# Gaps in SBUF that set where the streamed operands of single-pass matmuls lie against the weights loaded beside them

## The chip, the cores and the metric

One core of one Trainium2 chip runs the whole program. The metric is device time in microseconds (us), lower is better. TensorE's matmul array is PE, its weight loads are PEld; DVE is VectorE, ACT is ScalarE, POOL is GpSimd, and SP is the queue that issues most loads.

## The reference

256 tokens of 1,024 values pass through a first block (a mixer of attention and a state recurrence, then product-key experts) and a second block of two layers (feed-forward, mixer, feed-forward each). All is float32. The parts with most products:

```python
def peer_ffn(h, w_query, sub_keys1, sub_keys2, expert_u, expert_v):
    q = x @ w_query                                    # 8 heads, top 16 of 128*128 experts each
    ...
    u = jnp.take(expert_u, ic, axis=0)
    act = jax.nn.gelu(jnp.einsum('cd,ced->ce', xc, u))
    vv = jnp.take(expert_v, ic, axis=0)
    return jnp.einsum('ce,ced->cd', gc * act, vv)

def swiglu(h, w_gate, w_up, w_down):                   # four of them; 1024 x 2816, 2816 x 1024
    return (jax.nn.silu(h @ w_gate) * (h @ w_up)) @ w_down
```

## The kernel before

Every large product is made of single-pass matmuls in the type float32r, whose operands are split in two parts that add up to the float32 value: `mm3` (L105 to L107) issues three matmuls, of high by high, high by low and low by high part. One matmul loads 128x128 weights into the array and streams an operand [128, 256] past them, the transposed activations of all 256 tokens (in `proj_n` the roles are swapped). While one streams, the weights of the next are loaded, so at any time two places of SBUF are read for TensorE: the streamed operand of this matmul and the weights of the next.

The stages, in order of time, with the streamed operand and the weights by their tile names:

- `first_half`: the products with `w_in` (`xh`, `xl` against `wh`, `wl`), then the recurrence, attention and `w_out` (`qk..`, `zr..` against `wh`, `wl`), woven together.
- `peer`: the query products (`xh`, `xl` against `wh`, `wl`). Then the **u stage**, 128 blocks of 128 experts each: SP loads a block of `peer_u` (tile `u`, two buffers), DVE transposes it (`uT`), ACT and POOL split it (`uh`, `ul`, three buffers), and PE does 24 matmuls (`ph`, `pl` against `uh`, `ul`). Beside it DVE finds the best keys, and from the middle on `spread` builds the gates from one-hot tiles (`one`, DVE and ACT), multiplies them on PE (L1148, two-pass float32 matmuls of 128 columns) and applies them (`G`, DVE). DVE, ACT and POOL keep their written order here. Then the **v stage**, again 128 blocks of 24 matmuls (L1291 to L1293): SP loads two blocks at a time (tile `v`, two buffers, L1270), ACT, DVE and POOL split them (`vh`, `vl`, L1277 and L1278), ACT and DVE split the gated activations (`ah`, `al`), and PE streams `ah`, `al` against `vh`, `vl`. All eight sums stay in PSUM through the stage.
- The second block: `ffn` four times. Its gate and up products stream `xh`, `xl` (44 groups of 24 matmuls), its down product streams `hh`, `hl` (528 matmuls, L1340 on, eight sums in four pairs). Between them the mixers (`mxh`, `mxl`; `grr`, `gir`).

Tiles come from pools that lie one behind the other in a partition; a pool's memory is given to the next pool when it closes, and an instruction that writes a tile waits for the readers and writers of whatever lay there before. So the size of every tile ahead of another in a pool sets that tile's address, and with it what its first write waits for. The order of instructions on an engine is set by the tile scheduler and, within `peer`, by the program.

Of the kernel before, what the change touches and what calls it, by code (L numbers as in the profile page):

```python
# [26 lines left out]
HOLD = 1.5  # L27
HALVES = slice(0, 64), slice(64, 128)


class K:
    """What the parts of the program share."""
# [30 lines left out]
    def pw(self, shape):  # L63
        """A bank from both of the working tags in turn."""
        self.turn = (self.turn + 1) % 3
        return self.psum(shape, tag="o", bufs=2) if self.turn == 2 else self.psum(shape)

    def raws(self, es, bufs=3):
        """Room for weights as they come, as long as es lasts."""
        self.raw = es.enter_context(self.tc.tile_pool(reuse_waits="tile", name="raw", bufs=bufs))  # L70

    def splits(self, es, bufs=3, width=1024):
        """Room for the parts of weights, as long as es lasts."""
# [9 lines left out]
    def load(self, src, k0, nk, n0, n):  # L83
        """Rows k0*128.. of src [K, N], columns n0..n0+n, with the rows on partitions."""
# [7 lines left out]
    def split(self, v):  # L92
        """Two parts that add up to the weights [128, nk, n]."""
# [8 lines left out]
    def mm3(self, out, sh, sl, mh, ml, first, last):  # L102
        """out += s.T @ m from the parts of both."""
# [9 lines left out]
    def columns_of(self, R, name):  # L113
        """R, the same in every partition, with the tokens on partitions: [128, 2]."""
# [13 lines left out]
class Rms:  # L128
    """1/sqrt(mean(x^2) + eps) over the rows of xT, the same in every partition: [128, T]; chunk by chunk as x comes."""
# [6 lines left out]
    def chunk(self, c):  # L136
# [12 lines left out]
        if c == self.early:  # L149
            # the table that the root needs  # L150
# [20 lines left out]
class Norm(Rms):  # L171
    """x * g in two parts, and what rmsnorm scales the tokens by; if by4 the parts' tokens are chunked()."""
# [24 lines left out]
class Last:  # L197
    """The rows of x by tokens, rmsnorm and the way out."""
# [9 lines left out]
    def chunk(self, c):  # L208
# [8 lines left out]
        if c == 6:  # L217
            # the table that the root needs
# [15 lines left out]

def weave(nc, tasks):
    """Emits generators side by side: of those whose last step should be through first, the first in the list takes its next
    step. tasks are (name, generator, names it comes behind)."""
# [33 lines left out]
# ---------------------------------------------------------------- first block  # L271
def columns(k, pool, rows, name, eng=None):
    """Vectors as rows of 128 -> columns over partitions."""
# [16 lines left out]
def vec(ap):  # L290
    """A flat vector of n*128 as [n, 128]."""
    return ap.rearrange("(n p) -> n p", p=128)


def modulation(k, pool, px):
    """silu(c) @ ada_w + ada_b, as columns [128, 48]: the first third, and generators for the others."""
# [59 lines left out]
def modulated(k, pool, tmp, g, shift, scale, R):  # L356
    """x R g (1 + scale) + shift in two parts."""
# [15 lines left out]
def proj_t(k, w, xh, xl, n0, n, use, nk=8, k0=0):  # L373
    """(x @ w[:, n0:n0+n]).T in chunks of 128 rows: use(chunk, psum [128, T])."""
# [20 lines left out]
def proj_n(k, w, xh, xl, n0, n, use, nk=8):  # L395
    """x @ w[:, n0:n0+n] by token tiles: use(tile, column, psum [128, 256])."""
# [20 lines left out]
def rsqrt(k, new, p, scale, eps):  # L417
    """1/sqrt(scale*p + eps), or of max(p, eps) without a scale; one Newton step behind the table."""
# [13 lines left out]
def masks(k, keep, pool):  # L432
    """Triangles within blocks of 64 and, for each doubling of the inverse, its off-diagonal blocks (and the diagonal)."""
# [41 lines left out]
def head_sums(k, xs, out):  # L475
    """Sums over each head's 64 rows of [128, 4, T]: [8, T]."""
# [4 lines left out]
def head_bcast(k, y, c, out, start=True, stop=True, **kw):  # L481
    """Row 2c and 2c+1 of [8, T] over the two heads of chunk c."""
# [3 lines left out]
def dilated_bias(k, keep, pool):  # L486
    """|t - key| and the log of how many of the patterns take the pair."""
# [61 lines left out]
def token_shift(k, pool, p, c, mu, out):  # L549
    """z + mu_prev (z_before - z) + mu_next (z_after - z), along the free axis."""  # L550
# [12 lines left out]
class Pair:  # L563
    """Two heads of the state recurrence: chunks of 64 steps; the second direction's time runs backwards."""
# [1527 lines left out]
```

## Time and profile before

| what | before |
|---|---|
| time, median of 3 runs (lowest to highest) | 2401.83 us (2395.73 to 2407.34) |
| span of the profiled execution | 2396.3 us |
| PE busy, PEld busy | 2257.4 us (94%), 2136.7 us (89%) |
| DVE, ACT, POOL busy | 1804.0, 1275.7, 852.5 us |
| chain that ended last | PE 66%, DVE 18%, issue 6%, DMA 4% |

The profiled execution has a span and no time of its own beside it; its span lies within the three timed runs and 5.5 us under their median. In a view by stretches a row gives the stretch in us from the start of the span, its length, then for PE, PEld, DVE, ACT and POOL the busy time with the number of instructions that touch the stretch, then PEclk (the clock that TensorE was granted, 1.00 is 2.4 GHz and 0.50 is 1.2 GHz), the busy share of the DMA engines and their GB/s. One record of a matmul with 256 columns lasts 0.28 us and laps over the next two, so a stretch of W us in which PE never stops is touched by (W + 0.28) / pace matmuls, where pace is the time from one start to the next.

### The profile page before, as it was taken

Reading aid. Unit: us, or ns where it says so; the run is one execution under the profiler, and the core shown is the slowest. Engines: PE = TensorE matmul, PEld = TensorE weight load, DVE = VectorE, ACT = ScalarE, POOL = GpSimd, SP = SyncE. Lnnn points to the kernel's source line nnn. Section 1 sums busy time; section 2 is a strip of 40 time slices with the busy share of each in tenths; the row PEclk is TensorE's granted clock in tenths of the full one; section 3 lists DMA queues with packets and bytes.
Section 4 is the critical chain, followed back from the end, with each engine's and each line's share of the span. In section 5 each row is a group of like instructions: output and inputs, shape, how many; then the busy total and the mean of one; then the engine's idle time right before and its main releaser. Section 6 shows DMA issues by size and latency. Waiting matters only on the chain.

```text
span 2396.3 us, 46806 instructions
## 1 busy us (share of the span) xinstructions
PE 2257.4 (94%) x17962; PEld 2136.7 (89%) x17962; DVE 1804.0 (75%) x3277; ACT 1275.7 (53%) x2691; POOL 852.5 (36%) x816
## 2 busy tenths in 40 slices
PE   7999998888899999999999999999999999989998
PEld 4877686888799998999999999987999999979998
DVE  7888786898789999677777666667876566687664
ACT  4543433644577776455555554445646666536543
POOL 2132210678778777444444300110352231141000
PEclk8999799899999999999999999999999999989999
DMA  7422122355555554555545566521655455515653
GB/s 261 158 89 89 36 79 90 117 132 149 143 141 142 140 135 127 174 183 179 191 176 188 167 217 197 167 80 45 191 180 177 158 176 185 185 49 170 209 194 115
DMA packets 299232, 358.38 MB, mean 150 GB/s; under 512 B 19324, under 2 KB 271680, under 8 KB 297984
## 3 DMA queue, kind: packets, MB, share of 16 engines
q1 hardware_dynamic: 290432, 349.52, 46.3%
q10 hardware_dynamic: 8032, 5.54, 0.8%
q8 instruction: 141, 2.31, 0.4%
q0 software_dynamic: 544, 0.33, 0.1%
q14 instruction: 83, 0.68, 0.1%
HBM read 354.28 MB, written 1.05 MB: 148 GB/s over the span
## 4 chain that ended last, share of the span: by engine, by line
PE 66%; DVE 18%; issue 6%; DMA 4%; POOL 3%; ACT 2%; SPq 1%; DVEq 0%; POOLq 0%; ACTq 0%
PE g L105 9%; PE g L107 9%; PE g L106 9%; PE o L105 3%; PE o L106 3%; DVE uT L992 3%; PE o L107 3%; DMA u<-in_peer_u_dram 3%; PE o L1293 3%; PE o L1292 3%; PE y L1291 2%; PE y L1293 2%; PE o L1291 2%; PE y L1292 2%; DVE one L992 2%
## 5 line engine op out<-in xcount | busy, mean ns | idle before, releaser
L98 ACT ACTIVATE wh<-raw 128x1024 fp32r<-128x1024 f32 (+3 forms) x397 | 386.9, 977 | 396.1 <-PE g L106 198.9
L99 DVE TENSOR_TENSOR wl<-raw,wh 128x1024 fp32r<-128x1024 f32 (+3 forms) x381 | 431.3, 1134 | 221.0 <-ACT wh L98 205.6
L105 PE MATMUL g<-xh,wh 128*128 128x256 f32 x1864 | 529.6, 285 | 5.4 <-ACT xh L367 3.0
L107 PE MATMUL g<-xh,wl 128*128 128x256 f32 x1864 | 525.8, 283 | 8.7 <-DVE wl L99 8.6
L106 PE MATMUL g<-xl,wh 128*128 128x256 f32 x1864 | 525.3, 282 | 5.3 <-DVE xl L368 2.9
L992 POOL TENSOR_TENSOR ul<-uT,uh 128x512 fp32r<-128x512 f32 x256 | 363.6, 1445 | 108.2 <-ACT uh L992 104.0
L105 PEld LDWEIGHTS g<-xh,wh 128*128 128x128 f32 x1864 | 357.4, 192 | 11.9 <-issue 3.8
L107 PEld LDWEIGHTS g<-xh,wl 128*128 128x128 f32 x1864 | 356.3, 191 | 12.4 <-DVE wl L99 11.8
L106 PEld LDWEIGHTS g<-xl,wh 128*128 128x128 f32 x1864 | 356.4, 191 | 7.4 <-DVE xl L368 3.7
L107 PE MATMUL g<-ph,ul 128*128 128x256 f32 x1024 | 295.9, 289 | 14.2 <-POOL ul L992 14.1
L105 PE MATMUL g<-ph,uh 128*128 128x256 f32 x1024 | 297.3, 290 | 6.0 <-ACT uh L992 6.0
L106 PE MATMUL g<-pl,uh 128*128 128x256 f32 x1024 | 294.0, 287 | 0.0
L1277 ACT ACTIVATE vh<-v 128x512 fp32r<-128x512 f32 x256 | 147.2, 623 | 178.6 <-POOL vl L1278 86.5
L1278 POOL TENSOR_TENSOR vl<-v,vh 128x512 fp32r<-128x512 f32 x128 | 165.3, 1292 | 206.1 <-ACT vh L1277 204.2
L107 PEld LDWEIGHTS g<-ph,ul 128*128 128x128 f32 x1024 | 198.1, 193 | 18.9 <-POOL ul L992 18.9
L105 PEld LDWEIGHTS g<-ph,uh 128*128 128x128 f32 x1024 | 198.4, 194 | 6.9 <-ACT uh L992 6.8
L105 PE MATMUL o<-hh,wh 128*128 128x256 f32 x704 | 198.1, 281 | 1.5 <-DVE t L1348 1.5
L106 PEld LDWEIGHTS g<-pl,uh 128*128 128x128 f32 x1024 | 198.2, 194 | 0.0
L106 PE MATMUL o<-hl,wh 128*128 128x256 f32 x704 | 197.7, 281 | 0.0
L107 PE MATMUL o<-hh,wl 128*128 128x256 f32 x704 | 197.4, 280 | 0.0
L992 ACT ACTIVATE uh<-uT 128x512 fp32r<-128x512 f32 x256 | 147.2, 624 | 92.7 <-DVE uT L992 92.0
L125 DVE TENSOR_TENSOR al<-G,ah 128x256 fp32r<-128x256 f32 x128 | 170.6, 1334 | 16.6
(775 smaller groups left out, 5672.7 us busy)
## 6 DMA issues: line engine op xcount, KB each, us to landing
u<-in_peer_u_dram SPq DMA_DIRECT2D x512, 128.0 KB, 2.9
v<-in_peer_v_dram SPq DMA_DIRECT2D x64, 1024.0 KB, 4.8
raw<-in_ffn_w_gate_dram SPq DMA_DIRECT2D x44, 1024.0 KB, 5.9
raw<-in_ffn_w_up_dram SPq DMA_DIRECT2D x44, 1024.0 KB, 5.3
raw<-in_ffn_w_down_dram SPq DMA_DIRECT2D x32, 1024.0 KB, 5.1
raw<-in_ada_w_dram SPq DMA_DIRECT2D x24, 1024.0 KB, 5.1
raw<-in_w_in_dram SPq DMA_DIRECT2D x13, 1024.0 KB, 5.2
raw<-in_ffn_w_down_dram SPq DMA_DIRECT2D x16, 768.0 KB, 4.4
```

What stands on the lines that cost most here:

```text
L98: nc.scalar.activation(h, v, AF.Copy)
L99: self.sub.tensor_tensor(l, v, h.bitcast(F), op=OP.subtract)
L105: nc.tensor.matmul(out, sh, mh, start=first, stop=False)
L106: nc.tensor.matmul(out, sh, ml, start=False, stop=False)
L107: nc.tensor.matmul(out, sl, mh, start=False, stop=last)
L125: self.nc.vector.tensor_sub(l, src, h.bitcast(F))
L992: return lambda *args, **kw: self.tc.keep_in_program_order(f(*args, **kw))
L1277: nc.scalar.activation(vh[:, s], r[:, s], AF.Copy)
L1278: eng.tensor_tensor(vl[:, s], r[:, s], vh[:, s].bitcast(F), op=OP.subtract)
L1291: nc.tensor.matmul(o, vh[:, s], ah, start=i == 0 and c % 2 == 0, stop=False, skip_group_check=True)
L1292: nc.tensor.matmul(o, vh[:, s], al, start=False, stop=False, skip_group_check=True)
L1293: nc.tensor.matmul(o, vl[:, s], ah, start=False, stop=i == NB - 1, skip_group_check=True)
```

## The change

A helper `gap` takes a tile of a given number of bytes out of a pool, writes one column of it with a POOL MEMSET, and is called ahead of the streamed operands of nearly every stage with a size from the table `GAPS`. In the v stage the six tiles `ah`, `al` are now taken once, ahead of the pool's other tiles, with a gap on either side of them, and used in turn; before, they were three buffers each behind `vl`. No matmul is added or removed, and none changes its place in PE's order; the same holds for DVE, ACT and SP. POOL gets 13 MEMSETs of 128x1. (Comments were removed too; line numbers shift by 1 to 18.)

```diff
+GAPS = dict(w_in=416, w_out=448, query=64, u=64, v=448, ffn=(32, 128, 128, 448), even=416, odd=448, glu=256)
...
+def gap(k, pool, size, name="gap"):
+
+    if size:
+        k.nc.gpsimd.memset(pool.tile([128, size // 4], F, name=name, bufs=1)[:, 0:1], 0.0)
...
+            gap(k, pz, GAPS["w_in"])
...
+            gap(k, k.spl, GAPS["w_out"])
...
+        gap(k, part, GAPS["query"])
...
+        gap(k, pool, GAPS["u"])
...
         vs = {}
+        gap(k, pool, GAPS["v"])
+        ahl = [[pool.tile([128, T], FR, name=f"{x}{i}") for i in range(3)] for x in ("ah", "al")]
+        gap(k, pool, 512 - GAPS["v"], "gap2")
...
-            ah, al = (pool.tile([128, T], FR, name=x, bufs=3) for x in ("ah", "al"))
+            ah, al = (x[i % 3] for x in ahl)
...
+        gap(k, pool, GAPS["ffn"][2 * l + j])
...
+        gap(k, pool, GAPS["even"])
...
+        gap(k, pool, GAPS["odd"])
...
+        gap(k, pool, GAPS["glu"], "gap2")
```

What it does to the addresses, read from the layouts of the two built programs: the offset of the streamed operand from the weights, modulo 512 bytes. Weights of one matmul and the next lie a multiple of 512 bytes apart within a stage, so a stage has one offset.

| stage | streamed | matmuls | before | now |
|---|---|---|---|---|
| `w_in` | `xh`, `xl` | 528 | 32 | 448 |
| `w_out` (7 of 8 row blocks) | `qk`, `zr` | 168 | 384 | 448 |
| query | `xh`, `xl` | 384 | 0 | 448 |
| u stage | `ph`, `pl` | 3072 | 0 | 448 |
| v stage | `ah`, `al` | 3072 | 0 | 448 |
| down product, 1st ffn | `hh`, `hl` | 528 | 416 | 448 |
| down product, 2nd and 3rd ffn | `hh`, `hl` | 1056 | 320 | 448 |
| down product, 4th ffn | `hh`, `hl` | 528 | 0 | 448 |
| even mixer, out | `mxh`, `mxl` | 192 | 32 | 448 |
| odd mixer, out | `mxh`, `mxl` | 192 | 0 | 448 |
| odd mixer, glu | `grr`, `gir` | 96 | 256 | 448 |
| gate, up and other products of the second block | `xh`, `xl` | 4680 | 448 | 448 |

One thing that engines wait for moves with the addresses: what the loads of the v stage wait for, since the tiles `v` now lie over other tiles of the u stage. SP's queue at the end of the u stage, before (each row an instruction, out<-in and the semaphores that it waits for):

```order
L1169 DMA u<-in_peer_u_dram 32x4x256 x3
L1270 DMA v<-in_peer_v_dram 128x2x1024 [waits DMAHW0_49,DVE_49,PE_49]
L1270 DMA v<-in_peer_v_dram 128x2x1024 [waits DMAHW1_49,PE_49,Pool_49]
L1270 DMA v<-in_peer_v_dram 128x2x1024 [waits DMAHW0_49,DMAHW2_49,DVE_49,Pool_49]
L1270 DMA v<-in_peer_v_dram 128x2x1024 [waits DMAHW1_49,DMAHW3_49,DVE_49,Pool_49]
```

The same place now:

```order
L1180 DMA u<-in_peer_u_dram 32x4x256 x3
L1284 DMA v<-in_peer_v_dram 128x2x1024 [waits DVE_49,PE_49,DMAHW0_49,Activation_49,Pool_49]
L1284 DMA v<-in_peer_v_dram 128x2x1024 [waits DMAHW1_49]
L1284 DMA v<-in_peer_v_dram 128x2x1024 [waits DMAHW0_49,DMAHW2_49,DVE_49,Pool_49]
L1284 DMA v<-in_peer_v_dram 128x2x1024 [waits DMAHW1_49,DMAHW3_49,DVE_49,Pool_49]
```

The first load's wait for PE was for the last gate matmul of `spread` (L1148), three blocks ahead of the end of the u stage; it is now for the last matmul of the stage (`ph` against `ul`), which before only the second load waited for.

POOL's queue around the same place, before:

```order
L992 TENSOR_TENSOR ul<-uT,uh 128x512 [waits Activation_49]
L1278 TENSOR_TENSOR vl<-v,vh 128x512 [waits DMAHW2_49,DMAHW1_49,DMAHW3_49,DMAHW0_49,Activation_49]
L1278 TENSOR_TENSOR vl<-v,vh 128x512 [waits DMAHW5_49,DMAHW6_49,DMAHW4_49,DMAHW7_49,Activation_49,Pool_49]
L1278 TENSOR_TENSOR vl<-v,vh 128x512 [waits DMAHW1_49,Activation_49]
L1278 TENSOR_TENSOR vl<-v,vh 128x512 [waits PE_49,DVE_49,Activation_49,Pool_49]
```

and now:

```order
L1001 TENSOR_TENSOR ul<-uT,uh 128x512 [waits Activation_49]
L239 MEMSET gap 128x1
L239 MEMSET gap_11695 128x1
L1292 TENSOR_TENSOR vl<-v,vh 128x512 [waits DMAHW4_49,DMAHW2_49,DMAHW5_49,DMAHW1_49,DMAHW6_49,DMAHW0_49,DMAHW7_49,Activation_49,Pool_49]
L1292 TENSOR_TENSOR vl<-v,vh 128x512 [waits PE_49,Activation_49,Pool_49]
```

Two MEMSETs stand between the last `ul` and the first `vl`. The other eleven stand at the starts of their stages, and what they wait for was finished earlier in the program.

## Rows read from the trace of the kernel before

**Rows 1.** Page, busy time by engine: busy us (share of the span) xinstructions.

```profile
PE 2257.4 (94%) x17962; PEld 2136.7 (89%) x17962; DVE 1804.0 (75%) x3277; ACT 1275.7 (53%) x2691; POOL 852.5 (36%) x816
```

**Rows 2.** Stretches: u stage in four parts, then the v stage.

```profile
487.00:663.00 176.00, 151.69 (x1165) 145.77 (x1164) 147.10 (x382) 81.70 (x173) 138.07 (x109) 0.96 0.57 148
663.00:905.00 242.00, 237.63 (x1961) 235.03 (x1960) 222.91 (x309) 179.79 (x528) 192.84 (x129) 1.00 0.54 139
905.00:958.00 53.00, 47.54 (x386) 46.53 (x387) 52.89 (x65) 32.92 (x101) 36.26 (x25) 1.00 0.47 122
958.00:971.00 13.00, 10.77 (x88) 10.54 (x87) 7.45 (x11) 4.87 (x14) 7.56 (x6) 1.00 0.34 112
971.00:1344.00 373.00, 370.81 (x3074) 370.23 (x3072) 261.86 (x261) 187.50 (x386) 166.10 (x132) 1.00 0.52 183
```

**Rows 3.** Stretches in which PE never stops: v stage, and the fourth down product.

```profile
990.00:1090.00 100.00, 100.00 (x836) 100.00 (x835) 71.62 (x70) 50.60 (x105) 44.99 (x35) 1.00 0.52 182
2340.00:2353.00 13.00, 13.00 (x110) 13.00 (x110) 6.28 (x7) 4.90 (x6) 0.00 (x0) 1.00 0.52 171
```

**Rows 4.** The same view: four stretches of gate and up products.

```profile
2215.00:2315.00 100.00, 100.00 (x885) 100.00 (x884) 67.31 (x94) 50.34 (x74) 0.00 (x0) 1.00 0.61 195
1372.00:1427.00 55.00, 55.00 (x488) 55.00 (x487) 36.33 (x51) 27.91 (x41) 0.00 (x0) 1.00 0.72 226
1939.00:1959.00 20.00, 20.00 (x173) 20.00 (x172) 12.96 (x20) 13.44 (x27) 6.69 (x12) 1.00 0.61 195
1999.00:2019.00 20.00, 20.00 (x172) 20.00 (x171) 12.86 (x19) 13.31 (x28) 6.70 (x12) 1.00 0.61 193
```

**Rows 5.** The same view: down products of the first, second (two stretches) and third ffn.

```profile
1480.00:1500.00 20.00, 20.00 (x172) 20.00 (x172) 11.32 (x14) 10.03 (x14) 1.69 (x2) 1.00 0.54 183
1869.00:1882.00 13.00, 13.00 (x113) 13.00 (x112) 7.78 (x11) 6.92 (x10) 1.50 (x2) 1.00 0.67 223
1885.00:1898.00 13.00, 13.00 (x117) 13.00 (x116) 7.03 (x9) 6.03 (x9) 2.23 (x2) 1.00 0.71 236
2036.00:2056.00 20.00, 20.00 (x172) 20.00 (x172) 13.22 (x18) 10.12 (x14) 2.25 (x2) 1.00 0.54 178
```

**Rows 6.** Waits of PE between 487 and 663: us in total, times, longest us.

```profile
PE g L107 <- POOL ul L992: 14.1, 21, 1.0
PE g L105 <- ACT uh L992: 6.0, 4, 3.1
```

**Rows 7.** Waits of PE between 663 and 905.

```profile
PE g L1148 <- ACT one L992: 3.9, 8, 1.0
```

**Rows 8.** Stretch 663 to 905, the instructions that read `pl` alone.

```profile
663.00:905.00 242.00, 148.85 (x520) 99.60 (x520) 0.00 (x0) 0.00 (x0) 1.00 0.54 139
```

**Rows 9.** Timeline around 971: start, us, engine, line, out<-in; SP, PE, then ACT.

```profile
962.58 9.06 SPq L1270 DMA_DIRECT2D v<-in_peer_v_dram  x2
...
970.90 0.28 PE L107 MATMUL g<-ph,ul 128*128 128x256 f32 x1
973.08 0.38 PE L1291 MATMUL o<-ah,vh 128*128 128x256 f32 x1 [1.90 <-ACT vh L1277]
...
971.50 1.01 ACT L124 ACTIVATE ah<-G 128x256 fp32r<-128x256 f32 x3
972.41 2.18 ACT L1277 ACTIVATE vh<-v 128x512 fp32r<-128x512 f32 x4
976.26 1.15 ACT L1277 ACTIVATE vh<-v 128x512 fp32r<-128x512 f32 x2 [1.67 <-DMA v<-in_peer_v_dram]
```

**Rows 10.** Loads of `v`, from issue to landing.

```profile
DMA to landing us min/median/max: 4.7/4.8/5.8
```

**Rows 11.** Stretches after the 1.9 us stop, then around a 6.7 us stop.

```profile
974.00:978.00 4.00, 4.00 (x22) 4.00 (x22) 2.04 (x2) 1.74 (x4) 3.10 (x3) 0.57 0.48 181
...
2136.00:2142.00 6.00, 0.00 (x0) 0.00 (x0) 5.20 (x6) 0.35 (x1) 2.52 (x3) 0.67 0.00 0
2142.00:2150.00 8.00, 7.50 (x34) 6.24 (x35) 6.84 (x12) 1.66 (x4) 3.59 (x5) 0.61 0.01 2
```

## The prediction

> **What bounds the kernel now.** I read the busy times first: PE is busy for 94% of the span, no other engine for more than 75% [rows 1]. But a busy PE only says that matmuls follow each other, so the next question is how fast they follow. The view by stretches answers it where PE never stops: touched matmuls give the pace, (W + 0.28) / count. In the v stage that is 100.28 / 836 = 119.95 ns [rows 3]; in the gate and up products of the fourth ffn 100.28 / 885 = 113.3 ns [rows 4]. The instruction is the same in both, 128x128 weights and 256 columns at full clock, so 6.6 ns of each matmul in the v stage are no arithmetic. The table of offsets in the section on the change goes with it: the v stage has offset 0, the gate and up products have 448.
>
> Whether the offset does it is best seen where nothing else differs. The down product is the same code in all four ffn, at three offsets. At 0 it runs at 13.28 / 110 = 120.7 ns [rows 3], at 416 at 20.28 / 172 = 117.9 ns, at 320 at 117.5 and 117.9 ns in two stretches and at 13.28 / 117 = 113.5 ns in a third [rows 5]. The last matters: one offset shows two paces, about 113.4 and 117.7, and between the second and the third of these stretches stand only four matmuls of the next norm, of another offset. The gate and up products at 448 show the same pair: 113.3 in two stretches of 100 and 55 us, 117.2 and 117.9 in two others [rows 4]. So I read an offset as what decides which paces are to be had, and a stop of PE, or a few other matmuls in between, as what picks one of them, which then lasts to the next such place. At 448, uninterrupted stretches of the fast pace add up to some 350 us and of the slow one to some 116 us, by the same view (two of each are shown), so three quarters are fast and the mean is 0.75 x 113.3 + 0.25 x 117.6 = 114.4 ns. At 0 I find the fast pace in no stretch that I read.
>
> **The change part by part.** It brings 9,816 single-pass matmuls to offset 448; 4,680 were there.
>
> *v stage.* 3,072 matmuls in 373 us, PE busy 370.8, DVE 261.9, ACT 187.5, POOL 166.1 [rows 2]: PE alone bounds it. At 0 it holds 119.95 throughout. It runs without a stop and without other matmuls, so it takes one pace for all of it. Fast: 3,072 x (119.95 - 113.3) = 20.4 us less. Slow (117.6): 7.2 us. I take the fast one, the likelier. The others can follow: at 113.3 a block takes 2.72 us, DVE needs 261.9 / 128 = 2.05 of them, and a load of two blocks lands in 4.8 us [rows 10] against 5.4.
>
> *u stage.* The matmuls would save up to 3,072 x (119.95 - 114.4) = 17.0 us, but PE is not alone here. From 663 to 905 it is busy 237.6 of 242 us and waits only 3.9 [rows 2, 7]; 3 x 520 of the matmuls lie there [rows 8], worth 8.7 us. DVE is at 222.9 of 242 in that part, with 19 us to spare, so it could take the speed-up in full only if its waits shrank in step; I take 5 of the 8.7. From 905 to 958 DVE is busy 52.9 of 53 us [rows 2]: nothing. Before 663 PE already waits 20 us for POOL and ACT [rows 6], whose work comes behind DVE's: I take 1. Together 6, bounds 0 and 17.
>
> *Down products.* PE does not stop for other engines there. First ffn: 528 x (117.9 - 114.4) = 1.8 us; second and third: 1,056 x (117.2 - 114.4) = 3.0, with 117.2 between the three stretches of rows 5; fourth: 528 x (119.95 - 114.4) = 2.9. Together 7.7.
>
> *The small stages.* Offsets 0 and 256 (query, odd mixer, glu): 672 matmuls x 5.5 = 3.7 us, with 256 taken as 0. Offsets 32 and 384 (`w_in`, `w_out`, even mixer): 888 x 3.1 = 2.8 us, by the nearest rows, those at 416 and 320 [rows 5]. These stages stop often for other engines, so between 0 and 6.5; I take 4.5.
>
> *Gate and up products.* Their offset stays, but each stop deals the pace anew, and stops will fall elsewhere. All fast would give 4,680 x 1.1 = 5 us, half of them slow would cost 5. I take 0.
>
> *The first load of v.* Here the change costs. It was issued at 962.58 and had landed long before the u stage ended at 971.18; PE began at 973.08, behind ACT's `ah` and `vh` [rows 9]. Now it waits for the last matmul of the u stage. That very wait is in the trace, on the second load: ACT could begin its `vh` at 976.26 [rows 9]. From a `vh` to PE's start are 973.08 - 972.41 = 0.67 us, so PE would start at 976.93, 3.9 us later; with the longest landing of 5.8 [rows 10] 4.8. The stop grows from 1.9 to 5.8 us, and PE then runs at half clock for longer: over 974 to 978 the clock was 0.57 [rows 11], half clock for 3.4 us; behind a stop of 6.7 us it was 0.61 over 8 us [rows 11], half clock for 6.2. Each such us loses half of itself: 0 to 1.4 us more, I take 1. Together 4.9, bounds 3.5 and 6.2. Queued behind the first load on SP is only the second, which had the same wait already. The third waits for POOL's `vl` of the second block and shifts by the same 4 us, as do its users.
>
> *The MEMSETs.* 13 small writes on POOL, which is idle for 64% of the span [rows 1]; what they wait for is long past, and the two before the v stage stand where POOL waits for `vh` anyway. Nothing; if POOL were late there, they would delay the first `vl` by what two one-column writes take.
>
> Sum: -20.4 - 6 - 7.7 - 4.5 + 4.9 = -33.7 us. The profiled execution has a span of 2396.3, which gives 2362.6; the median of the runs lies 5.5 us above the span, so I put the sum on the median: 2401.8 - 33.7 = 2368.
>
> **The rivals.** *The v stage takes the slow pace:* 7.2 in place of 20.4, which gives 2381. For it: a quarter of the time at 448 is slow. Against: the longest stretches at 448 are fast [rows 4]. 20%.
>
> *The offset is not the cause* and each stage keeps its pace; then only the late load is left, 2401.8 + 4.9 = 2407. For it: what else differs between stages (tiles, buffers, other engines' traffic) changes with them. Against: the four down products [rows 3, 5]. 5%. The Trainium skill speaks for this rival, in "SBUF — State Buffer", section "Who interferes with whom": TensorE has two independent read ports, one for the moving operand and one for weight loads, and "PE and ACT never wait on anyone". By that rule addresses change nothing and the result is this rival's; rows 3 to 5 show 113.3 to 120 ns for one and the same instruction, so the trace does not agree.
>
> *Slower: most stops deal the slow pace.* If all 14,496 matmuls ran at 117.6, the gate and up products would lose 4,680 x (117.6 - 114.4) = 15.0 us, the v stage would gain 7.2, the u stage 2.5, the rest 2, and the late load cost 4.9: 8 us slower, 2410. Each tenth of fast share is worth 0.43 ns x some 12,000 matmuls that count = 5.2 us, so it decides below a fast share of 0.16. For it: nothing shows what picks the pace. Against: three quarters now. 3%.
>
> *The u stage gives all of its 17 us:* 2357. DVE at 53 of 53 us stands against it. 4%.
>
> **How the numbers follow.** Likeliest, with 68%: 2368, by itself 2358 to 2378 (u stage 0 to 10, small stages 0 to 6.5, gate and up +-5, load 3.5 to 6.2). The range takes in the slow v stage and the full u stage with some of that scatter: 2354 to 2388; the two cases of no effect and of slow pace, 8%, lie above it. A measurement of this kernel tells about 0.5%, 12 us, from no change. Faster by more than that (below 2390) are the first, the slow v stage and the full u stage, 92%, less 2 for scatter of the second; within it the two upper rivals, 8%; beyond 2414 only both late load and slow pace at their worst, 2%.
>
> **What would show it.** Right: the v stage about 353 us long from first to last matmul, with 885 and not 836 matmuls in 100 us; the fourth down product at 113 to 118 ns; a stop of PE near 5.8 us at the start of the v stage with a DMA wait of ACT before it; the u stage within 10 us of its 484. Wrong: the pace at 448 in the v stage stays at 120 (no effect); or a third pace appears; or the u stage shrinks by more than 10 us, which would say that DVE's busy time there was waiting for PE.

## The result and the profile after

The changed kernel takes 2375.2 us (median of 4 runs, 2370.8 to 2383.2) against 2399.1 us for the kernel before beside it: the ratio is 0.989, interval 0.986 to 0.992. In a second comparison (the run `after_again` below) it takes 2383.9 us against 2404.0, ratio 0.991, interval 0.989 to 0.994. The forecast was 2368, range 2354 to 2388: the sign and the main cause came out, and about 10 of the 34 us forecast did not, 14 by the second comparison. That both medians lie within the range owes something to luck, since two of the ten executions of the changed kernel, at 2388.7 and 2393.2 us, lie above it.

The busy times by engine, from the page of the changed kernel, answer to [rows 1]. PE loses 38 us and the other engines keep theirs:

```profile
PE 2219.6 (94%) x17962; PEld 2096.6 (88%) x17962; DVE 1801.2 (76%) x3277; ACT 1275.3 (54%) x2691; POOL 853.1 (36%) x829
```

The same stretches as in [rows 2, 3], changed kernel:

```profile
487.00:663.00 176.00, 147.17 (x1151) 140.03 (x1150) 145.74 (x383) 81.11 (x171) 136.61 (x108) 0.96 0.58 146
663.00:905.00 242.00, 232.46 (x1976) 229.62 (x1974) 221.17 (x310) 180.92 (x530) 194.73 (x132) 1.00 0.56 142
905.00:958.00 53.00, 48.33 (x392) 47.33 (x392) 52.89 (x67) 33.93 (x102) 36.21 (x25) 0.97 0.47 120
...
990.00:1090.00 100.00, 100.00 (x885) 100.00 (x884) 75.83 (x75) 54.03 (x111) 47.62 (x38) 1.00 0.55 192
...
2317.00:2329.00 12.00, 12.00 (x108) 12.00 (x108) 5.45 (x7) 4.49 (x9) 0.00 (x0) 1.00 0.68 219
```

In the v stage 885 matmuls touch 100 us where 836 did: 113.3 ns in place of 119.95. The fourth down product runs at 12.28 / 108 = 113.7 ns in place of 120. The u stage shows no such gain: in the same 242 us 1,976 matmuls in place of 1,961, and PE is busy for 232.5 us in place of 237.6. PE got faster there and waits more; and from 905 to 958 its granted clock is 0.97, where it was 1.00 [rows 2].

Where the time went is read from the starts of the same matmul in the two traces (PE's order is the same in both):

| place | before, us | after, us | shift |
|---|---|---|---|
| first matmul of the u stage | 486.9 | 486.9 | 0.0 |
| last of the u stage | 970.9 | 970.9 | 0.0 |
| first of the v stage | 973.1 | 976.9 | +3.8 |
| last of the v stage | 1343.5 | 1327.1 | -16.4 |
| first of the 1st down product | 1476.9 | 1460.7 | -16.2 |
| first of the 2nd | 1832.9 | 1813.7 | -19.2 |
| first of the 3rd | 2033.2 | 2013.1 | -20.1 |
| first of the 4th | 2320.7 | 2300.1 | -20.6 |
| last of the 4th | 2385.6 | 2362.0 | -23.6 |

The v stage gives 20.2 us, the late load takes 3.8, all the rest together gives some 7, and the 970 us up to the end of the u stage give nothing. This is one trace against one. In the twelve traces with the changed addresses the u stage begins anywhere from 484.7 to 493.2 us, so a gain of 2 or 3 us ahead of it could not be seen in this way.

The start of the v stage in the timeline of the changed kernel (start, us, engine, line, out<-in, idle before and its end; SP, POOL, ACT, then PE), beside [rows 9]:

```profile
971.35 13.50 SPq L1284 DMA_DIRECT2D v<-in_peer_v_dram  x4
...
965.22 0.13 POOL L239 MEMSET gap<- 128x1 f32 x2
...
971.53 1.02 ACT L125 ACTIVATE ah<-G 128x256 fp32r<-128x256 f32 x3
976.21 2.19 ACT L1291 ACTIVATE vh<-v 128x512 fp32r<-128x512 f32 x4 [3.66 <-DMA v<-in_peer_v_dram]
...
976.89 0.58 PE L1305 MATMUL o<-ah,vh 128*128 128x256 f32 x1 [5.68 <-ACT vh L1291]
```

The first load leaves at 971.35 behind the last u matmul, ACT's `vh` waits 3.66 us for it, and PE's stop is 5.68 us in place of 1.90. The two MEMSETs took 0.13 us, long before POOL was needed.

### The profile page after: what moved, and what is told of

It reads as the page before. It is cut to its first block, busy times and chain, and to the rows that moved or that the text cites. A ratio compares the mean times of both kernels' runs of the same rounds, so it can differ in the third digit from the quotient of the medians.

```text
span 2372.7 us, 46823 instructions
## 1 busy us (share of the span) xinstructions
PE 2219.6 (94%) x17962; PEld 2096.6 (88%) x17962; DVE 1801.2 (76%) x3277; ACT 1275.3 (54%) x2691; POOL 853.1 (36%) x829
## 4 chain that ended last, share of the span: by engine, by line
PE 64%; DVE 18%; DMA 6%; issue 4%; ACT 3%; POOL 3%; SPq 2%; DVEq 0%; ACTq 0%; POOLq 0%
PE g L106 8%; PE g L108 8%; PE g L107 8%; DMA u<-in_peer_u_dram 4%; DVE uT L1001 4%; PE o L106 3%; PE o L107 3%; PE o L108 3%; PE o L1305 2%; PE o L1306 2%; PE o L1307 2%; PE y L1306 2%; PE y L1305 2%; PE y L1307 2%; DVE one L1001 2%
## 5 line engine op out<-in xcount | busy, mean ns | idle before, releaser
L126 DVE TENSOR_TENSOR al<-G,ah 128x256 fp32r<-128x256 f32 x128 | 171.5, 1341 | 16.2
```

The source lines that it names most:

```text
L126: self.nc.vector.tensor_sub(l, src, h.bitcast(F))
```

## The experiments

"Offset" is always the streamed operand less the weights, modulo 512 bytes.

### Is it the offset? The same layout with the offsets at 0

```diff
-GAPS = dict(w_in=416, w_out=448, query=64, u=64, v=448, ffn=(32, 128, 128, 448), even=416, odd=448, glu=256)
+GAPS = dict(w_in=480, w_out=512, query=512, u=512, v=512, ffn=(96, 192, 192, 512), even=480, odd=512, glu=256)
...
-        gap(k, pool, 512 - GAPS["v"], "gap2")
+        gap(k, pool, 512, "gap2")
```

> The changed kernel with gaps of other sizes: all 9,816 matmuls that the change brought to offset 448 lie at offset 0, and every tile, MEMSET and wait stays as in the change. If the offset is the cause: 119.95 ns in the v stage and in all four down products, so against the kernel before the u and v stages gain nothing, the first three down products lose some 1,584 x 2.4 ns = 4 us, w_in, w_out and the even mixer up to 888 x 2.5 ns = 2 us, and the late load costs its 4 to 5: about 2411 us. If it is something else that the change brought (tiles in one piece, gaps, other addresses as such): 113.3 ns in the v stage, and about 2375.

Measured: 2410.6 us against 2403.7 for the kernel before beside it, ratio 1.0028 (1.0012 to 1.0044). By the layout of the built program the 168 matmuls of `w_out` are not at 0 but at 384, as before the change; the stages that are read here are at 0. Stretches of its trace in the v stage and the first down product:

```profile
990.00:1090.00 100.00, 100.00 (x835) 100.00 (x835) 71.22 (x71) 50.99 (x105) 44.60 (x35) 1.00 0.53 183
...
1490.00:1510.00 20.00, 20.00 (x169) 20.00 (x169) 10.14 (x13) 9.66 (x14) 1.68 (x2) 1.00 0.54 178
```

100.28 / 835 and 20.28 / 169 are both 120 ns. With everything of the change in place but the offsets, the gain is gone and the costs are left: the v stage starts 3.4 us later than in the kernel before, and the four down products together take 261.4 us in place of 257.6. The offset is the cause.

A rival is that not the offset but the address of one of the two operands counts. The layouts and the paces exclude it. Modulo 512 bytes, the weights of the v stage lie at 416 before and after the change, at 119.95 and at 113.3 ns. A streamed operand lies at 416 in the v stage before, at 119.95 ns, and also in the u stage of the changed kernel, whose weights lie at 480. There the fast pace shows in stretches without a stop, 7.68 / 68 = 113 ns where the kernel before has 7.68 / 64 = 120; first the kernel before, then the changed one:

```profile
513.50:520.90 7.40, 7.40 (x64) 7.40 (x63) 7.19 (x20) 2.65 (x7) 5.41 (x6) 1.00 0.49 142
```

```profile
513.50:520.90 7.40, 7.40 (x68) 7.40 (x67) 7.16 (x22) 2.80 (x7) 5.87 (x5) 1.00 0.54 142
```

What in the memory or in the array makes the offset count, no run shows.

### Is the late load worth its 4 to 5 us?

```diff
-        gap(k, pool, GAPS["v"])
-        ahl = [[pool.tile([128, T], FR, name=f"{x}{i}") for i in range(3)] for x in ("ah", "al")]
-        gap(k, pool, 512 - GAPS["v"], "gap2")
+        ahl = []
...
+            if i == 0:
+                gap(k, pool, GAPS["v"])
+                ahl.extend([pool.tile([128, T], FR, name=f"{x}{n}") for n in range(3)] for x in ("ah", "al"))
             ah, al = (x[i % 3] for x in ahl)
```

> The changed kernel with the six tiles ah, al and their gap taken behind v, vh and vl, so that v lies where it lay before the change and its first load no longer waits for the last matmul of the u stage; the offset stays 448. My theory (the late load costs what the v stage starts later): PE starts the v stage some 2 us after the end of the u stage and not 5.9, and the time falls by 4 to 5 us from 2375.2, to about 2371; pace in the v stage 113.3 ns (or 117.6, were the stop's length to pick the other one, which would give 2384). Rival (the clock after the stop or another transfer takes the gain back): start earlier, but the end of the v stage within 1 us of that of the changed kernel, 2375.

Measured: the first load leaves at 959.82 again, and the timeline shows PE's stop at 1.91 us:

```profile
959.82 25.20 SPq L1282 DMA_DIRECT2D v<-in_peer_v_dram  x5
...
971.43 0.39 PE L1306 MATMUL o<-ah,vh 128*128 128x256 f32 x1 [1.91 <-ACT vh L1289]
```

The v stage lasts 349.5 us from first to last start (changed kernel 350.2), so in these two traces the late load cost 3.8 us of stop and 0.7 of slower first blocks, and the rival, by which the gain is taken back within the stage, is out. The traced execution took 2367.3 us, 7.4 less than the traced one of the changed kernel. The times do not show the gain: the five executions lay between 2367.3 and 2393.2 with a median of 2381.4 (ratio 0.992, 0.989 to 0.995), above the 2375.2 that was to be undercut. Something worth 26 us differs from one execution to the next.

### What differs between executions

> The same kernel as early_load a second time, for its trace: its runs lay between 2367 and 2393 us, and the trace was that of the fastest. If an execution deals the paces anew: the v stage at 117.8 ns in this trace, or other stretches of gate and up products at another pace than in the first trace, and the time differs by what they cost (v stage 13 us). If the pace belongs to the program: the same pace everywhere and the spread has another cause.

Measured: 2393.95 us. The v stage in the first and in the second trace of this same kernel:

```profile
1000.00:1300.00 300.00, 300.00 (x2650) 300.00 (x2649) 226.18 (x221) 161.23 (x332) 143.55 (x111) 1.00 0.57 194
```

```profile
1000.00:1300.00 300.00, 300.00 (x2549) 300.00 (x2549) 216.83 (x213) 155.19 (x320) 136.43 (x106) 1.00 0.54 187
```

300.28 / 2650 = 113.3 ns and 300.28 / 2549 = 117.8 ns, same program, same addresses, same full clock. The v stage is 363.7 us long in place of 349.5; that is 14.2 of the 26.6 us by which the two spans differ. A part of the gate and up products before the fourth down product differs in the same way, 70.28 / 620 = 113.4 and 70.28 / 597 = 117.7 ns:

```profile
2200.00:2270.00 70.00, 70.00 (x620) 70.00 (x619) 46.88 (x65) 35.56 (x52) 0.00 (x0) 1.00 0.64 204
```

```profile
2220.00:2290.00 70.00, 70.00 (x597) 70.00 (x596) 44.91 (x63) 34.17 (x50) 0.00 (x0) 1.00 0.59 185
```

So the addresses do not fix the pace. The two traces were taken on different chips (numbers 5 and 8 on record), so this pair by itself cannot tell execution from chip; but on chip 8 as on chip 12 the v stage at 448 was traced at both paces, in different kernels. Of the eight traces in which the v stage starts at 448 behind a stop and stays there, six have the fast pace and two the slow one.

> The changed kernel itself once more, for the spread of its executions and a second trace. If an execution deals the paces anew: a spread of some 15 to 25 us, median 2375 to 2385, and in the trace some stretches at 448 with another pace than in the first trace. If the program fixes them: the same paces in the same places, and executions within 0.3% of 2375.

Measured: 2383.9 us, six runs from 2374.3 to 2393.2, ratio 0.991 (0.989 to 0.994). In the second trace the v stage is fast again (350.1 us long), but the span is 12.3 us longer. Of that, 6.3 us had come together before the u stage, which begins at 493.2 in place of 486.9, and 8.2 by the start of the v stage; the rest comes between the first and the third down product (the same matmuls start 8.3 us later at the one and 12.9 at the other). The largest step lies in the query products, where PE waits longer for `G`; the waits between 470 and 500 in the first and in the second trace:

```profile
PE g L1076 <- DVE G L1238: 0.7, 1, 0.7
```

```profile
PE g L1076 <- DVE G L1238: 2.9, 1, 2.9
```

With the longer stop the granted clock fell to half: over 477 to 484 it is 0.51, and 1.00 in the first trace. The mean granted clock goes with the times of this run as a whole. The two executions of 2374.3 and 2376.3 us have 0.969, the four from 2380.9 to 2393.2 have 0.962 to 0.964; in `early_load` the two fastest have 0.971 and 0.972, the other three 0.965 to 0.967. By estimate, 0.006 less over 2,385 us are 29 us at half clock, which cost up to 14 us. So the spread has two parts that the record shows, the pace and the granted clock; whether other causes make PE stop and the clock only follows, no run tells apart.

### Which offset gives which pace

```diff
-        ahl = [[pool.tile([128, T], FR, name=f"{x}{i}") for i in range(3)] for x in ("ah", "al")]
+        ahl = [[pool.tile([128, T + 128], FR, name=f"{x}{i}") for i in range(3)] for x in ("ah", "al")]
...
-            ah, al = (x[i % 3] for x in ahl)
+            c0 = (i // 8 * 32 + 64) % 512 // 4
+            ah, al = (x[i % 3][:, c0:c0 + T] for x in ahl)
```

> The changed kernel with the six tiles ah, al of 384 columns in place of 256, of which every 8 blocks of the v stage use another 256: the offset is 0 for blocks 0 to 7, 32 for blocks 8 to 15, and so on by 32 to 480. If the offset decides the pace: 119.95 ns at 0 and 256, 117.6 or 113.3 at 32, 64, 320, 384, 416, and at 448 113.3 or 117.6; for the other offsets the traces have no row. The v stage is then some 3,072 x 117.5 ns = 361 us long. If a stage keeps one pace that is dealt at its start: one pace in all 16 pieces.

> The same with the offsets in falling order, 480 for blocks 0 to 7 down to 0 for blocks 120 to 127. If an offset has one pace: the same pace for each offset as in the rising order. If an offset allows two and the piece before decides which: 0 and 256 at 119.95 in both orders, but 113.3 in the one and 117.6 in the other for some of 64, 320, 384, 416, 448.

Measured: matmuls that touch 20 us within each piece of the v stage, at full clock but for the first piece of each order; 20.28 us over the count gives the pace: 169 are 120.0 ns, 171 118.6, 172 117.9, 173 117.2, 174 116.6, 179 113.3.

| offset | 0 | 32 | 64 | 96 | 128 | 160 | 192 | 224 | 256 | 288 | 320 | 352 | 384 | 416 | 448 | 480 |
|---|---|---|---|---|---|---|---|---|---|---|---|---|---|---|---|---|
| rising | (164) | 173 | 172 | 169 | 171 | 173 | 172 | 171 | 169 | 172 | 172 | 169 | 171 | 172 | 172 | 172 |
| falling | 169 | 174 | 172 | 169 | 170 | 171 | 172 | 171 | 169 | 173 | 179 | 169 | 171 | 173 | 179 | (167) |

The rows for 256, 320 and 448 in the rising order, then for 448, 320 and 256 in the falling order:

```profile
1168.00:1188.00 20.00, 20.00 (x169) 20.00 (x168) 13.30 (x15) 10.06 (x22) 9.20 (x7) 1.00 0.59 208
...
1214.00:1234.00 20.00, 20.00 (x172) 20.00 (x171) 14.62 (x15) 10.22 (x21) 9.24 (x8) 1.00 0.58 208
...
1305.00:1325.00 20.00, 20.00 (x172) 20.00 (x172) 14.60 (x15) 10.22 (x21) 9.25 (x8) 1.00 0.58 207
```

```profile
1003.00:1023.00 20.00, 20.00 (x179) 20.00 (x178) 15.11 (x15) 11.14 (x24) 9.15 (x8) 1.00 0.62 210
...
1094.00:1114.00 20.00, 20.00 (x179) 20.00 (x178) 15.28 (x16) 10.35 (x22) 10.04 (x8) 1.00 0.60 207
...
1138.00:1158.00 20.00, 20.00 (x169) 20.00 (x168) 14.24 (x15) 10.07 (x22) 9.03 (x7) 1.00 0.58 206
```

The whole v stage lasts 366.1 and 364.3 us, where 361 were expected. Two things are to be seen. In the rising order the values repeat after 256 bytes, within one matmul of the count: 0 and 256, 96 and 352 are the worst at 120, and the others lie between 117.2 and 118.6. And 113.3 appears at 320 and 448 only, in one order and not in the other: both paces belong to one offset. Smaller differences between the orders show at other offsets too (173 and 171 at 160, 173 and 174 at 32). Whether what ran before decides, or the execution, these two traces cannot tell, since they are of two kernels and of one execution each.

### What picks the pace at 448

```diff
+            c0 = (((0, 416, 480)[i // 8 % 3] if i % 8 < 2 else 448) + 64) % 512 // 4
+            ah, al = (x[i % 3][:, c0:c0 + T] for x in ahl)
```

> The changed kernel with ah, al of 384 columns; of every 8 blocks of the v stage the last 6 are at offset 448 and the first 2 at another one, in turn 0, 416 and 480, so that the pace at 448 is picked anew 16 times, behind three different offsets. If the pick is by what ran before: all pieces behind one of the offsets alike, for instance 113.4 behind 480 and 117.8 behind 416, as in the falling and the rising order. If it is chance with the shares seen in the kernel before: some 12 of 16 at 113.4, mixed behind every offset. The v stage then takes some 3,072 x 115.5 ns = 355 us.

Measured: all 16 pieces at 448 run at 113.3, behind 0, 416 and 480 alike, and the v stage takes 354.3 us. In this trace, pieces behind 416 and behind 480, 14.28 / 126 = 113.3 ns each:

```profile
1012.00:1026.00 14.00, 14.00 (x126) 14.00 (x125) 10.61 (x11) 7.70 (x17) 6.61 (x6) 1.00 0.63 221
...
1034.00:1048.00 14.00, 14.00 (x126) 14.00 (x125) 10.62 (x11) 7.66 (x17) 6.58 (x6) 1.00 0.65 222
```

Neither expectation holds. Chance with a share of three quarters, drawn anew for each piece, gives 16 of 16 once in a hundred; and "what offset ran before" falls too, since 448 behind 416 was slow in the rising order above. That something is carried along from piece to piece within an execution would fit all of these traces. It was not tested by itself, and what it would be, no run here shows.

A version with the early load that goes through offset 0 for two of every 32 blocks tries to use this:

```diff
...
+            c0 = 16 if i % 32 < 2 else 0
+            ah, al = (x[i % 3][:, c0:c0 + T] for x in ahl)
```

> The kernel early_load (first load of v early, offset 448), with tiles ah, al of 384 columns and the first 2 of every 32 blocks of the v stage at offset 0. Behind 0 all 6 pieces at 448 of v_deal ran at 113.3. If a piece at 0 sets the fast pace: the v stage at 113.3 but for those 8 blocks in every execution, 351 us in the trace, and no executions with the slow one, so about 2372 and a spread that is 14 us narrower than that of early_load (2367 to 2393). If the pick is chance in each execution: pieces at 117.8 in the trace, or the same spread as early_load's.

Measured: 2374.9 us, ratio 0.9885 (0.9864 to 0.9907), all four pieces fast in its trace (v stage 351.3 us), and four runs within 2371.3 to 2379.2, against 2367.3 to 2393.2 for `early_load` and 2374.3 to 2393.2 for the changed kernel beside it. That is what the expectation asked for, but four runs are few, and its interval and the changed kernel's (0.9885 to 0.9939) overlap: that it beats the changed kernel is not shown, and neither is that offset 0 sets the pace, since the v stage at 448 was fast in six of eight traces without it.

### Why the u stage gained nothing

From its first to its last matmul the u stage lasts 484.0 us before and 483.5 in `all_zero`, both at offset 0. At 448 it lasts 484.0 in the changed kernel and 482.9 to 487.0 in the seven other traces of kernels that leave it as it is. The first try to take other engines out of its way:

```diff
-                us[j] = pool.tile([128, 1024], F, name="u", bufs=2)
+                us[j] = pool.tile([128, 1024], F, name="u", bufs=4)
...
-            uT = pool.tile([128, 1024], F, name="uT", bufs=2)
...
-            V.transpose(uT, us[j].rearrange("p (g b i) -> p b g i", g=4, b=8))
-            for b in (0, 512):
+            uT = us[j]
+            for b, E in ((0, V), (512, P)):
...
-                P.tensor_tensor(l[:, s], uT[:, s], h[:, s].bitcast(F), op=OP.subtract)
+                E.tensor_tensor(l[:, s], uT[:, s], h[:, s].bitcast(F), op=OP.subtract)
```

> The changed kernel (u stage at offset 448) with its u stage relieved: the transposes uT on DVE are left out, so u is split as it was loaded (four buffers of u in the place of uT), and half of the subtractions ul goes from POOL to DVE. By the mean durations in the changed kernel DVE has 157 us less and some 88 more, POOL 181 less. If the u stage gained nothing because DVE and POOL set its pace, PE bounds it now: of its waits only some microseconds are left, and it lasts less than 484 us by far more than 10, and 10 to 20 less than with offset 0 (next run). If the pace of these matmuls gives nothing in this stage, whatever the other engines do: the same length as with offset 0, within 3 us.

> The same with the gap of the u stage at 512 bytes, that is with its streamed operands at offset 0. If DVE and POOL were what hid the gain: 3,072 matmuls at 119.95 in place of a mean of 114.4 ns, the u stage 10 to 20 us longer than in the run before. Otherwise the same within 3 us.

Measured: 543.7 us at 448 and 538.3 at 0, longer than the stage had been. The edit was a bad one: the half of `ul` that went to DVE waits for ACT's `uh`, and everything behind it in DVE's queue waits with it. The waits of DVE from 663 to 905 in `u_bare_448`:

```profile
DVE ul L1001 <- ACT uh L1001: 81.4, 49, 2.4
```

The changed kernel has no such wait. So the pair says nothing on the question; it shows only that the stage grew by some 54 to 60 us with this wait in DVE's queue. The second try leaves every wait as it is and makes DVE's instruction smaller:

```diff
-            V.transpose(uT, us[j].rearrange("p (g b i) -> p b g i", g=4, b=8))
+            V.transpose(uT[:, :512], us[j][:, :512].rearrange("p (g b i) -> p b g i", g=4, b=4))
...
-                A.activation(h[:, s], uT[:, s], AF.Copy)
-                P.tensor_tensor(l[:, s], uT[:, s], h[:, s].bitcast(F), op=OP.subtract)
+                A.activation(h[:, s], uT[:, :512], AF.Copy)
+                P.tensor_tensor(l[:, s], uT[:, :512], h[:, s].bitcast(F), op=OP.subtract)
```

> The changed kernel (u stage at offset 448) in which DVE transposes only one half of each block of u, and ACT and POOL split that half twice: DVE has some 128 x 0.6 = 79 us less in the u stage, every wait has the same shape, and PE's matmuls are all there. If DVE is what hid the faster pace there: with the first gates at 650 us in both, the part behind them, 307 us long before, is 4 to 11 us shorter than with offset 0 (next run); the matmuls at 119.95 and at a mean of 114.8 ns differ by 2,016 x 5.2 ns = 10.4 us there. If something else holds it: within 2 us of it.

> The same with the gap of the u stage at 512 bytes, offset 0. PE is busy for 296 of the 308 us behind the first gate in the kernel before, so with DVE relieved this part takes about 298 to 302 us, and 4 to 11 us more than in the run before if DVE had hidden the gain; the same length within 2 us if not.

Measured, from the first gate matmul to the end of the stage, all with the same 2,528 matmuls: one stretch each of the kernel before, the changed kernel, `u_half_0` and `u_half_448`.

```profile
650.00:971.00 321.00, 308.86 (x2528) 305.02 (x2528) 291.77 (x395) 226.10 (x668) 242.86 (x163) 0.99 0.52 134
```

```profile
651.00:971.00 320.00, 303.59 (x2528) 299.75 (x2528) 288.11 (x395) 226.14 (x666) 241.69 (x165) 0.98 0.51 131
```

```profile
639.00:961.00 322.00, 310.56 (x2528) 306.21 (x2528) 267.34 (x395) 221.86 (x667) 244.32 (x165) 0.99 0.52 130
```

```profile
642.00:959.50 317.50, 303.18 (x2527) 298.05 (x2528) 266.22 (x395) 221.58 (x668) 245.54 (x165) 0.99 0.53 132
```

All waits of PE in that stretch (us in total, times, longest) are one line, here of the kernel before and of the changed kernel; in `u_half_0` it reads 15.4 us and in `u_half_448` 18.4.

```profile
PE g L1148 <- ACT one L992: 15.9, 16, 4.1
```

```profile
PE g L1158 <- ACT one L1001: 21.1, 17, 5.0
```

From the kernel before to the changed one, PE's busy time falls by 5.3 us and its wait for `one` grows by 5.2. With DVE relieved, offset 448 is worth 322.0 - 317.5 = 4.5 us in place of 1. Relieving DVE alone, at offset 0, is worth nothing (321 and 322). By the expectation DVE would hide a part, some 3.5 us. But each of these is one trace, and this same part lasts from 320.5 to 323.7 us in the eight traces that leave the u stage at 448 as it is, a scatter nearly as large; so that DVE hides a part is likely and not shown. Most of the 10.4 us that 2,016 faster matmuls would save still does not come through: the wait for `one` grows again, by 3.0. `one` is written by DVE, scaled by ACT and then read by PE; ACT itself waits for DVE's `one`, in the same stretch of the changed kernel:

```profile
ACT one L1001 <- DVE one L1001: 63.7, 64, 2.3
```

That this chain takes the rest is read from these waits and was not tried by itself. Neither were the loads of `u`, for which DVE waits between 663 and 905 as well, 6.5 us in the kernel before and 8.1 in the changed one.

The clock takes a part as well. In the kernel before, PE stops for 2.06 us and starts again at 906.90, at full clock; in the changed kernel it stops for 2.17 us, starts again at 905.94, and the clock is half until 909.3. The same 5 us, before and after:

```profile
905.00:910.00 5.00, 3.10 (x24) 3.10 (x25) 5.00 (x7) 2.96 (x9) 3.15 (x3) 1.00 0.44 116
```

```profile
905.00:910.00 5.00, 4.06 (x21) 4.06 (x22) 5.00 (x7) 2.96 (x9) 3.16 (x3) 0.66 0.40 110
```

From 960 to 965 the two clocks are again 1.00 and 0.66. Two stretches of 3.4 us at half clock that were not there before cost, by estimate, up to 3.4 us of the gain.

## Why the prediction was right or wrong

**Right: the offset is the cause.** With the same layout at offset 0 the time is 2410.6, 6.9 us above the kernel before; the expectation had about 9, from the late load and the stages that go to a worse offset. The rival "not the cause" (2407 for the changed kernel) is out. Here the traces do not agree with the Trainium skill, "SBUF — State Buffer", section "Who interferes with whom", by which PE's two read ports are independent and PE waits on no one: the same instruction took 113.3 and 120 ns in two layouts that differ in the offset.

**Right: the v stage.** PE alone bounds it, 113.3 and 119.95 ns came as forecast, and 370.5 - 350.2 = 20.3 us where the sum has 20.4. That this trace had the fast pace is in part luck: the forecast chose between two, and six of eight traces have the one it chose, which fits its odds and is too few to confirm them. An execution that draws the slow one is the rival at 2381. The ten executions of the changed kernel lie between 2370.8 and 2393.2, so a draw worth some 14 us is not all of the spread. That a stop of PE, or other matmuls in between, is what picks the pace, as the prediction read it, is not shown.

**Right: the late load's stop**, 3.8 us (forecast 3.9; the lower bound of 3.5 for the whole load followed from no row). The 1 us for clock cannot be told from nothing: against `early_load` the v stage is 0.7 us longer, but `all_zero` has the long stop and the offset of the kernel before, and its v stage is as long as that one's, 370.3 us and 370.5. Over 977 to 981 the granted clock of the changed kernel was 0.50, half, and with the early load's short stop 1.00 over 971.4 to 975.4. The kernel before, with a stop of the same 1.9 us, had 0.57 over 974 to 978 [rows 11], so the length of the stop alone does not settle the clock. Both stretches of the two traces:

```profile
977.00:981.00 4.00, 4.00 (x18) 3.93 (x19) 3.60 (x3) 2.56 (x5) 3.50 (x3) 0.50 0.25 101
```

```profile
971.40:975.40 4.00, 3.86 (x31) 3.66 (x32) 2.27 (x3) 2.42 (x5) 2.99 (x2) 1.00 0.58 239
```

**Wrong: the u stage**, 6 us forecast, 0 measured. The step that failed is the one that takes 5 of the 8.7 us between 663 and 905 because PE waits only 3.9 us there and DVE has 19 to spare. What the traces show in its place is that PE's busy time behind the first gate fell by 5.3 us and its wait for `one` grew by 5.2, and that the clock fell twice where it had been full. So DVE's spare time was no measure of what PE could gain: a faster PE came earlier to the end of a chain from DVE by ACT. That this chain is the whole cause is read from the waits and not shown. Few waits of an engine before a change do not say how many there will be after it.

**Mis-sized: the down products**, 7.7 us forecast. They take 257.6 us before and 252.2 in the first trace after, which gives 5.4; in the other eleven traces with offset 448 there the sum is 253.3 to 254.8, so 3 to 4 is the usual gain. The term that failed is the mean of 114.4 ns, taken from the gate and up products. The down products deal by a pattern of their own. Four stretches of the first one, one in each pair of its sums, in the changed kernel:

```profile
1462.00:1474.00 12.00, 12.00 (x108) 12.00 (x107) 5.87 (x7) 4.32 (x6) 0.00 (x0) 1.00 0.68 218
1477.00:1489.00 12.00, 12.00 (x108) 12.00 (x108) 6.26 (x8) 5.32 (x9) 0.82 (x2) 1.00 0.67 225
1493.00:1505.00 12.00, 12.00 (x104) 12.00 (x103) 5.57 (x8) 4.98 (x7) 0.75 (x1) 1.00 0.68 224
1508.50:1520.50 12.00, 12.00 (x104) 12.00 (x104) 5.68 (x6) 4.57 (x7) 2.04 (x2) 1.00 0.68 215
```

Two pairs are fast (12.28 / 108 = 113.7) and two slow (12.28 / 104 = 118.1). In the twelve traces it is fast, fast, slow, slow nine times and slow, slow, fast, fast three times, never anything else, so this product takes 61.6 us in all of them. The third one is the same in all twelve, nearly all slow, 64.0 us.

**Mis-sized: the small stages**, 4.5 us forecast. Up to the u stage nothing is to be seen (486.9 in both traces, 484.7 to 493.2 in the others), so what `w_in`, `w_out` and the query products gave is below the scatter; the mixers gave some 2 to 3 us in the first trace, and `after_again` lost as much there. The prediction had said that these stages stop for other engines and still took 4.5 of 6.5; what came lies nearer to its lower bound of 0.

**Right: the gate and up products** of the first ffn kept their mean in the first trace (-16.4 at the end of the v stage, -16.2 at the first down product). But the two traces of `early_load` show that an execution can lose some 4 us there (the shift between them is 22.9 us at the third down product and 26.6 at the fourth).

**Right: the MEMSETs** cost nothing: none of the 13 takes more than 0.3 us, and no instruction waits for one (ns, shortest, median and longest, then first and last start in us):

```profile
L239 POOL MEMSET gap<- x13: 88/98/297, 12.8 to 2132.7; 128x1 f32 x13
```

## What to carry to other kernels

Where matmuls follow each other without a stop, compare their start-to-start time between stages before looking for waits: here one instruction took from 113 to 120 ns by where its streamed operand lay against the weights, and moving the offset by 64 bytes gave 5% of a stage bound by PE alone. In a stage where PE waits even a little for a chain by another engine, price a faster PE near zero until a run shows more, as the u stage did here. And when tiles are moved for their addresses, look at what the first write of every tile moved with them now waits for.

## What the runs showed of the hardware that was not expected

- One program at one set of addresses has two paces of the same matmul at full clock, 113.3 and 117.8 ns, held for 3,072 matmuls on end: 14.2 us in the v stage between two executions of one kernel, on two chips. The executions of the kernel before, with no such pick in its u and v stages, lay between 2395.8 and 2410.1 in the last comparison, those of the changed kernel between 2374.3 and 2393.2.
- Executions of one program differ in the mean granted clock too, 0.962 to 0.969 within the six of `after_again`, and the slower four have the lower values. Behind a stop of 1.9 us at the same place the clock was 0.57 in one kernel and 1.00 in another.
- The pick shows patterns (fast, fast, slow, slow or its opposite in the first down product of twelve traces; 16 of 16 fast pieces in one execution; the same offset slow in another). What makes them stays open.
- In the v stage the slow values of the pace repeat every 256 bytes of offset in the rising order (120.0 at 0 and 256 and at 96 and 352, 117.2 to 118.6 elsewhere; 116.6 to 119.3 elsewhere in the falling one), while the fast pace was seen at 320 and 448 and not at 64 and 192.
